# Encoder layer on one core: standing zeros beside the queries, sums of squares in one column, eps as a column

## The chip, the cores and the metric

The kernel runs on one core of one Trainium2 chip. The metric is the time of one execution in device microseconds; the kernel before takes 1554.6 us (median of 3 runs, 1553.99 to 1555.76).

## What is computed

One layer of an encoder on x of 1024 tokens by 1024 channels, in float32. The part that the change touches is the differential attention (8 heads, two softmax maps a head, a head size of 64 for queries and keys, 128 for values):

```python
def head_rmsnorm(x, g):
    xf = x.astype(jnp.float32)
    return xf * lax.rsqrt(jnp.mean(xf * xf, axis=-1, keepdims=True) + EPS) * g.astype(jnp.float32)
...
    qn = head_rmsnorm(q, g_q) * (HEAD_DIM ** -0.5)
    kn = head_rmsnorm(k, g_k)
...
        s = jnp.einsum('bqhid,bkhid->bihqk', qblk, kn)
...
        s = jnp.where(allowed, s + bias, neg)
        p = jax.nn.softmax(s, axis=-1)
        a = p[:, 0] - lam * p[:, 1]
        return jnp.einsum('bhqk,bkhe->bqhe', a, vf)
...
    o = head_rmsnorm(o, g_sub) * (1.0 - lambda_init)
```

Ahead of it stand an RMSNorm and one projection to q, k, v and the pooling's channels; beside it a pooling mixer and the gates; behind it the branch products, the output projection and an MLP of 4096 channels with a squared ReLU.

## The kernel before

**Numbers in two halves.** Most matmuls work on fp32r operands. `split` (L115) makes two tiles of a float32 one: ScalarE casts the high half, VectorE (or GpSimd) subtracts it to give the low half. `mm3` (L120) then issues three matmuls, high by high, high by low and low by high, from the lines L123, L124 and L125. Nearly every projection in the trace is made of these three lines.

**Attention as a pipeline.** The tokens are 8 tiles of 128, so that 8 heads give 64 tiles, numbered g = 8h + t. For each g the loop at L645 runs stages of several tiles at once, each with its own lag (L48). `A` (`stage_qkv`) projects one tile into `z` in PSUM: 24 matmuls of 384 columns. `B` (`stage_prep`) squares q and k on ScalarE (L436), sums each of the four blocks of 64 on VectorE (L437), turns the sums into means with eps (L248) and takes the power -0.5 on GpSimd (L249); VectorE scales q and k (L441), GpSimd multiplies k by the gains (L447). `C` (`stage_qkT`) transposes them (L459, tile `tk`) and fills K and Q. The weights of a scores matmul have 128 rows for a head size of 64: the rows of one half hold q's high part against k's high part, the rows of the other half meet k's low part. So Q of each map is two tiles of weights: in the first, q's high part (L470) on its own rows and q's low part (L471) on the others; in the second, q's low part (L472) on its own rows and q (L473) on the others. `D` computes scores and softmax (tiles `sc`, `s`; L499 to L524), `E` transposes the weights of the values (tile `ta`, L555), `F` (`stage_pv`) multiplies them by V into the output `po` in PSUM, for a pair of tiles (256 queries) at a time, and stores it to DRAM unscaled.

**The sums of squares of the output.** ScalarE squares `po` into `oq` (L579), and `split` makes `oqs` of it, two halves. One step later `H` (`stage_ssq`) multiplies a 128x128 tile of ones by each half (L590, L591), 256 columns each, into the unused half of `po`'s bank. Each of the 128 rows of the result is then the same sum over the channels, and L593 takes its diagonal out with `identf`, one column of SS for each of the two tiles. `R` (`stage_norm`) makes the scales of a head from SS; they go to DRAM and are multiplied into the outputs when these are loaded for the branch product.

**Filling work.** The gates' columns (tile `g`) and the pooling's groups (`u`, `yp`) depend only on the normed x. They are written behind the attention in the code; the scheduler of the language, which runs a model of the engines, fills them in between the attention's instructions. A pooling group projects 512 tokens (`u`), copies the result to SBUF (L710), adds it to itself shifted by 1, 2, 4, 8 (L719; GpSimd copies the first columns, L718), subtracts (L728), splits (`mix`), and after one unit of the gates multiplies by the group's matrix (`yp`). A gate column loads its weights with two DMAs on SyncE's queue (`frgate`).

**Behind the attention** come the branch products (`bp`, `ba`), the output projection (`op`) and the MLP, which takes 7 products of half matrices in place of 8 (`X`, `Y`, `Z`, `W`, `Da`, `Db`). The change touches none of their lines.

Of the kernel before, what the change touches and what calls it, by code (L numbers as in the profile page):

```python
# [8 lines left out]
F32 = mybir.dt.float32  # L9
F32R = mybir.dt.float32r  # L10
I32 = mybir.dt.int32
AF = mybir.ActivationFunctionType
ALU = mybir.AluOpType
AX = mybir.AxisListType
# [3 lines left out]
P = 128  # L18
S = 1024
D = 1024  # L20
NT = S // P
NK = D // P
H = 8
HD = 64
POOLD = 512
WINDOWS = (2, 4, 8, 16)
EPS = 1e-6
# [7 lines left out]
N_Q, N_QN = 3, 2  # L35
# [20 lines left out]
def encoder_kernel(  # L56
# [21 lines left out]
    nc = tc.nc  # L78
    x, out = x[0], out[0]
# [4 lines left out]
    const = ctx.enter_context(tc.tile_pool(name="const", bufs=1))  # L84
# [15 lines left out]
    def htile(shape, dt, name, th):  # L100

        if th == 0:
            hcount[0] += 1
        return (hp1 if th else hp0[(hcount[0] - 1) // 4 % 2]).tile(shape, dt, tag="H", name=name)
# [7 lines left out]
    def f(ap):  # L112
        return ap.bitcast(F32)

    def split(hi, lo, src, lo_eng=None):  # L115

        nc.scalar.copy(hi, src)  # L117
        return (lo_eng or nc.vector).tensor_tensor(lo, src, f(hi), op=ALU.subtract)  # L118

    def mm3(ps, lhs_hi, lhs_lo, rhs_hi, rhs_lo, first, last, more=False):  # L120

        kw = {"skip_group_check": True} if more else {}
        nc.tensor.matmul(ps, lhs_hi, rhs_hi, start=first, stop=False, **kw)  # L123
        nc.tensor.matmul(ps, lhs_hi, rhs_lo, start=False, stop=False, **kw)  # L124
        nc.tensor.matmul(ps, lhs_lo, rhs_hi, start=False, stop=last, **kw)  # L125
# [101 lines left out]
    identf = const.tile([P, P], F32, name="identf")  # L227
    make_identity(nc, identf)
    mhalf = const.tile([P, NT], F32, name="mhalf")
    nc.gpsimd.memset(mhalf, -0.5)  # L230
    ones = const.tile([P, P], F32R, name="ones")
    nc.gpsimd.memset(f(ones), 1.0)
    inv = const.tile([P, 16], F32, name="inv")
    for i in range(16):
        nc.gpsimd.memset(inv[:, i : i + 1], 1.0 / (i + 1))
# [10 lines left out]
    def rsq(dst, ss, n, c):  # L246

        nc.vector.tensor_scalar(dst, ss, c, EPS, op0=ALU.mult, op1=ALU.add)  # L248
        nc.gpsimd.tensor_tensor(dst, dst, mhalf[:, :n], op=ALU.pow)  # L249
# [39 lines left out]
    with ExitStack() as ph:  # L289
        sp = ph.enter_context(tc.tile_pool(name="sp", bufs=1))  # L290
# [4 lines left out]
        def s1(shape, dt, name, tag, bufs=1):  # L295
            return sp.tile(shape, dt, tag=tag, name=name, bufs=bufs)
# [70 lines left out]
        gqk = sp.tile([P, 2, HD], F32, name="gqk")  # L367
        nc.sync.dma_start(gqk[:, 0, :], g_q[0].partition_broadcast(P))
        nc.sync.dma_start(gqk[:, 1, :], g_k[0].partition_broadcast(P))
        lqk = s1([P, 4, HD], F32, "lqk", "oq")  # L370
        nc.sync.dma_start(lqk, lambda_qk[0].partition_broadcast(P))

        dist = sp.tile([P, S], F32, name="dist")
# [13 lines left out]

        def small_params():
            nc.vector.scalar_tensor_tensor(
                gg, gqk[:, 0, :], HD ** -0.5, gqk[:, 1, :], op0=ALU.mult, op1=ALU.mult  # L390
            )
            nc.vector.tensor_tensor(lp, lqk[:, 0:4:2, :], lqk[:, 1:4:2, :], op=ALU.mult)
            nc.vector.tensor_reduce(ls, lp, axis=AX.X, op=ALU.add)
            nc.scalar.activation(ls, ls, AF.Exp)
            nc.vector.scalar_tensor_tensor(
                nlam, ls[:, 1:2], -LAMBDA_INIT, ls[:, 0:1], op0=ALU.add, op1=ALU.subtract
            )

        gg = sp.tile([P, HD], F32, name="gg")
# [4 lines left out]
        st = {}  # L404
        ATs = {}
        Zs = {}
        SS = {}

        gghs = {}

        def head_start(h):
            gghs[h] = sp.tile([P, HD], F32, tag="ggh", name=f"ggh{h}", bufs=2)
            nc.gpsimd.tensor_scalar(gghs[h], gg, -(2.0 ** (h + 1)), None, op0=ALU.mult)
            kv_tiles(h)
            Zs[h] = sp.tile([P, 2, NT], F32, tag="Z", name=f"Z{h}", bufs=2)
            SS[h] = sp.tile([P, NT], F32, tag="SS", name=f"SS{h}", bufs=2)
# [13 lines left out]
        def stage_prep(h, t):  # L430
            th = t // 4
            V, ggh = KV[h][1], gghs[h]
            z = st[h, t]["z"]
            sq = s1([P, 256], F32, f"sq{h}_{t}", "sq")
            ms = sp.tile([P, 4], F32, tag="ms", name=f"ms{h}_{t}", bufs=3)
            nc.scalar.activation(sq, z[:, 0:256], AF.Square)  # L436
            nc.vector.tensor_reduce(ms, sq.rearrange("p (a b) -> p a b", a=4), axis=AX.X, op=ALU.add)  # L437
            rsq(ms, ms, 4, 1.0 / HD)
            split(V[th][:, t % 4, 0, :], V[th][:, t % 4, 1, :], z[:, 256:384])
            qn = s1([P, 4, HD], F32, f"qn{h}_{t}", "qn", N_QN)  # L440
            nc.vector.tensor_tensor(  # L441
                qn,
                z[:, 0:256].rearrange("p (a b) -> p a b", a=4),
                ms.unsqueeze(2).broadcast_to([P, 4, HD]),
                op=ALU.mult,
            )
            nc.gpsimd.tensor_tensor(  # L447
                qn[:, 2:4, :], qn[:, 2:4, :], ggh.unsqueeze(1).broadcast_to([P, 2, HD]), op=ALU.mult
            )
            st[h, t] = {"qn": qn}  # L450
            yield

        def stage_qkT(h, t):

            th, c0 = t // 4, (t % 4) * P
            K, qn = KV[h][0][th], st[h, t]["qn"]
            tr = ps_t.tile([P, 512], F32, tag="tr", name=f"tk{h}_{t}")
            for i in range(2):
                nc.tensor.transpose(  # L459
                    tr[:, i * P : (i + 1) * P], qn[:, 2 * i : 2 * i + 2, :].rearrange("p a b -> p (a b)"), identf  # L460
                )
            Q = sp.tile([P, 2, 2, P], F32R, tag="Q", name=f"Q{h}_{t}", bufs=N_Q)
            halves = (slice(0, HD), slice(HD, P))
            for m in range(2):
                own, other = halves[m], halves[1 - m]
                q, k = tr[own, 0:P], tr[own, P : 2 * P]
                k_hi, q_hi = K[own, m, c0 : c0 + P], Q[own, m, 0, :]
                nc.scalar.copy(k_hi, k)
                nc.vector.tensor_tensor(K[other, m, c0 : c0 + P], k, f(k_hi), op=ALU.subtract)  # L469
                nc.scalar.copy(q_hi, q)  # L470
                nc.vector.tensor_tensor(Q[other, m, 0, :], q, f(q_hi), op=ALU.subtract)  # L471
                nc.vector.tensor_tensor(Q[own, m, 1, :], q, f(q_hi), op=ALU.subtract)  # L472
                nc.scalar.copy(Q[other, m, 1, :], q)  # L473
            st[h, t]["Q"] = Q
            yield

        def stage_scores(h, t):

            K, Q = KV[h][0], st[h, t]["Q"]
            n = (t + 1) * P  # L480
# [84 lines left out]
        def stage_pv(h, p):  # L565
            V, views = KV[h][1], ATs.pop((h, p))[0]
            po = ps_o.tile([P, 512], F32, tag="o", name=f"po{h}_{p}")
            nkt = 2 * p + 2
            for kt in range(nkt):
                v = V[kt // 4]  # L570
                mm3(
                    po[:, 0:256], v[:, kt % 4, 0, :], v[:, kt % 4, 1, :],
                    views[kt][0], views[kt][1], kt == 0, kt == nkt - 1,
                )
                if kt % 2 and kt < nkt - 1:
                    yield
            oS = s1([P, 256], F32, f"oS{h}_{p}", "oS", 2)
            oq = s1([P, 256], F32, f"oq{h}_{p}", "oq")
            nc.scalar.activation(oq, po[:, 0:256], AF.Square)  # L579
            nc.scalar.copy(oS, po[:, 0:256])  # L580
            nc.scalar.dma_start(y_dram[h * P : (h + 1) * P, p * 256 : (p + 1) * 256], oS)
            oqs = s1([P, 2, 256], F32R, f"oqs{h}_{p}", "oqs")
            split(oqs[:, 0, :], oqs[:, 1, :], oq)
            st[h, p, "o"] = (po, oq, oqs)
            yield

        def stage_ssq(h, p):

            po, oq, oqs = st.pop((h, p, "o"))
            nc.tensor.matmul(po[:, 256:512], ones, oqs[:, 0, :], start=True, stop=False)  # L590
            nc.tensor.matmul(po[:, 256:512], ones, oqs[:, 1, :], start=False, stop=True)  # L591
            for i in range(2):
                nc.vector.tensor_tensor_reduce(  # L593
                    out=oq[:, i * P : (i + 1) * P], in0=po[:, 256 + i * P : 256 + (i + 1) * P], in1=identf,
                    scale=1.0, scalar=0.0, op0=ALU.mult, op1=ALU.add,
                    accum_out=SS[h][:, 2 * p + i : 2 * p + i + 1],
                )
            yield

        def stage_norm(h):  # L600
# [14 lines left out]
            yield  # L615

        small_params()
        N = H * NT

# [25 lines left out]
        for g in range(-2, N + 8):  # L645
# [11 lines left out]
            for tok in ORDER:  # L657
                if tok not in gens:
                    i = g - tok[1]
# [151 lines left out]
    for d in range(NK):  # L811
# [10 lines left out]
        for th in range(2):  # L822
# [5 lines left out]
            t = htile([P, 2, 512], F32R, f"mT{d}_{th}", th)  # L828
# [495 lines left out]
```

## Time and profile before

| what | value |
| --- | --- |
| median of 3 runs | 1554.6 us |
| the profiled execution | 1553.41 us, its span 1551.6 us |
| granted TensorE clock | 1.00 |
| TensorE busy: matmul, weight load | 1533.6 us, 1320.8 us |
| VectorE, ScalarE, GpSimd busy | 1011.3, 816.7, 354.8 us |
| DMA | 206.94 MB, 133 GB/s in the mean |

The attention with its filling work lies from about 12 to 700 us, the branch products from 700 to 850, output projection and MLP behind that.

How to read it: PE is a matmul on TensorE, PEld its weight load, which can run beside the matmul before. DVE is VectorE, ACT ScalarE, POOL GpSimd, SP SyncE's queue. L590 is a line of the kernel. A group's row has line, engine, operation, output and inputs, shapes and count, then busy us and the mean ns of one, then the idle time of the engine ahead of them and what ended it. A row of the timeline has start, duration, engine, line. The end of a matmul is modelled and matmuls overlap, so that the step from one start to the next says what one costs in a dense stretch. A row of the waits has the total in us, how many, the longest.

### The profile page before, as it was taken

The page shows a single profiled execution, that of the slowest core. Times are in us where ns is not written, and L with a number is a line of the kernel's source. Part 1 is how long each engine was busy: PE and PEld are TensorE (multiplying, and loading weights), DVE is VectorE, ACT ScalarE, POOL GpSimd, SP SyncE. Part 2 cuts the span into 40 slices and gives each one's busy share as a digit, 9 for nine tenths or more (in the row PEclk, how much of TensorE's full clock was granted, in tenths as well). Part 3 has the DMA queues.
Part 4 walks back from the last instruction along what each step waited for, and adds up shares of the span by engine and source line. Part 5 has one row for each costly group of instructions (what it writes and reads, how often), then busy time and mean ns, then how long its engine had stood idle before and what let it go on. Part 6 is the DMA issues. An engine that isn't in the chain of part 4 may idle for free.

```text
span 1551.6 us, 22088 instructions
## 1 busy us (share of the span) xinstructions
PE 1533.6 (99%) x7649; PEld 1320.8 (85%) x7649; DVE 1011.3 (65%) x2277; ACT 816.7 (53%) x1810; POOL 354.8 (23%) x449
## 2 busy tenths in 40 slices
PE   7999999999999999999999999999999999999999
PEld 6999999999998989888888887888888788888887
DVE  7777677777878787746422458866665667556662
ACT  6656556656566555645532547565555633333331
POOL 5433334243525262324363400000000000000000
PEclk9999999999999999999999999999999999999999
DMA  7111212021202031248536534554343799437650
GB/s 229 51 53 48 66 41 68 24 75 37 75 28 83 28 96 42 69 147 284 179 122 210 168 112 124 182 185 155 129 142 109 278 334 370 170 122 257 224 190 27
DMA packets 168009, 206.94 MB, mean 133 GB/s; under 512 B 10117, under 2 KB 104026, under 8 KB 167898
## 3 DMA queue, kind: packets, MB, share of 16 engines
q1 hardware_dynamic: 150490, 178.23, 35.0%
q10 hardware_dynamic: 17408, 27.30, 4.7%
q8 instruction: 60, 0.98, 0.3%
q14 instruction: 51, 0.42, 0.1%
HBM read 150.94 MB, written 54.56 MB: 132 GB/s over the span
## 4 chain that ended last, share of the span: by engine, by line
PE 89%; DVE 4%; DMA 3%; ACT 1%; issue 1%; POOL 1%; SPq 0%; ACTq 0%; POOLq 0%; DVEq 0%
PE z L125 5%; PE z L123 5%; PE z L124 5%; PE Da L124 4%; PE Da L123 4%; PE Da L125 4%; PE g L123 3%; PE g L124 3%; PE g L125 3%; PE Db L124 3%; PE Db L123 3%; PE Db L125 3%; PE X L125 2%; PE X L123 2%; PE X L124 2%; PE sc L499 2%
## 5 line engine op out<-in xcount | busy, mean ns | idle before, releaser
L123 PE MATMUL z<-wqkv,hT 128*128 128x384 f32 x512 | 174.7, 342 | 0.4 <-DVE qn L441 0.3
L125 PE MATMUL z<-wqkv,hT 128*128 128x384 f32 x512 | 174.3, 341 | 0.5 <-DVE hT L118 0.5
L124 PE MATMUL z<-wqkv,hT 128*128 128x384 f32 x512 | 173.8, 339 | 0.0
L510 ACT ACTIVATE s<-s,nm 128x256 f32<-128x256 f32 (+7 forms) x128 | 99.6, 778 | 49.2 <-DVE nm L502 44.1
L249 POOL TENSOR_TENSOR ms<-ms,mhalf 128x4 f32<-128x4 f32 x64 | 66.6, 1040 | 157.7 <-DVE ms L248 139.1
L125 PE MATMUL g<-hT,fwgate 128*128 128x512 f32 x256 | 101.0, 394 | 0.0
L124 PE MATMUL g<-hT,fwgate 128*128 128x512 f32 x256 | 100.9, 394 | 0.0
L123 PE MATMUL g<-hT,fwgate 128*128 128x512 f32 x256 | 100.9, 395 | 0.0
L123 PEld LDWEIGHTS z<-wqkv,hT 128*128 128x128 f32 x512 | 96.9, 189 | 4.2 <-DVE qn L441 1.0
L125 PEld LDWEIGHTS z<-wqkv,hT 128*128 128x128 f32 x512 | 96.7, 189 | 3.3 <-DVE hT L118 1.3
L124 PEld LDWEIGHTS z<-wqkv,hT 128*128 128x128 f32 x512 | 96.8, 189 | 2.9
L502 DVE CUSTOM_DVE_ANT_0 s<-sc,dist 128x512 f32<-128x512 f32 (+3 forms) x128 | 74.7, 586 | 22.1 <-PE sc L500 20.7
L118 POOL TENSOR_TENSOR wqkv<-rqkv,wqkv 128x384 fp32r<-128x384 f32 x60 | 63.3, 1072 | 17.7 <-ACT wqkv L117 15.3
L499 PE MATMUL sc<-K,Q 128*128 128x512 f32 (+2 forms) x192 | 67.2, 355 | 0.1
L118 DVE TENSOR_TENSOR AS<-s,AS 128x512 fp32r<-128x512 f32 x64 | 43.8, 687 | 35.8 <-ACT AS L117 35.6
L500 PE MATMUL sc<-K,Q 128*128 128x512 f32 (+2 forms) x192 | 66.6, 354 | 0.0
L473 ACT CAST Q<-tk 64x128 fp32r<-64x128 f32 x128 | 33.2, 260 | 58.6 <-DVE Q L472 56.8
L447 POOL TENSOR_TENSOR qn<-qn,ggh 128x128 f32<-128x128 f32 x64 | 32.6, 510 | 137.5 <-DVE qn L441 124.2
L470 ACT CAST Q<-tk 64x128 fp32r<-64x128 f32 x128 | 33.1, 259 | 50.5 <-DVE K L469 49.1
L118 POOL TENSOR_TENSOR fwgate<-frgate,fwgate 128x512 fp32r<-128x512 f32 x32 | 45.2, 1416 | 52.2 <-ACT fwgate L117 52.0
L125 PEld LDWEIGHTS g<-hT,fwgate 128*128 128x128 f32 x256 | 48.1, 188 | 8.6
L123 PEld LDWEIGHTS g<-hT,fwgate 128*128 128x128 f32 x256 | 48.2, 188 | 7.1
(429 smaller groups left out, 4649.6 us busy)
## 6 DMA issues: line engine op xcount, KB each, us to landing
wd<-in_w_down_dram SPq DMA_DIRECT2D x56, 512.0 KB, 5.5
wu<-in_w_up_dram SPq DMA_DIRECT2D x32, 512.0 KB, 5.3
udS<-us SPq DMA_DIRECT2D x64, 256.0 KB, 2.5
ur<-udS SPq DMA_DIRECT2D x32, 512.0 KB, 3.2
rqkv<-in_w_in_dram SPq DMA_DIRECT2D x64, 192.0 KB, 2.8
ud<-u ACTq DMA_DIRECT2D x48, 256.0 KB, 2.2
ur<-ud SPq DMA_DIRECT2D x24, 512.0 KB, 5.5
frgate<-in_w_gate_dram SPq DMA_DIRECT2D x32, 256.0 KB, 2.6
```

Source lines behind the costliest of these rows:

```text
L118: return (lo_eng or nc.vector).tensor_tensor(lo, src, f(hi), op=ALU.subtract)
L123: nc.tensor.matmul(ps, lhs_hi, rhs_hi, start=first, stop=False, **kw)
L124: nc.tensor.matmul(ps, lhs_hi, rhs_lo, start=False, stop=False, **kw)
L125: nc.tensor.matmul(ps, lhs_lo, rhs_hi, start=False, stop=last, **kw)
L249: nc.gpsimd.tensor_tensor(dst, dst, mhalf[:, :n], op=ALU.pow)
L447: nc.gpsimd.tensor_tensor(qn[:, 2:4, :], qn[:, 2:4, :], ggh.unsqueeze(1).broadcast_to([P, 2, HD]), op=ALU.mult)
L470: nc.scalar.copy(q_hi, q)
L473: nc.scalar.copy(Q[other, m, 1, :], q)
L499: nc.tensor.matmul(dst, Q[:, i, 0, :], rhs, start=True, stop=False)
L500: nc.tensor.matmul(dst, Q[:, i, 1, :], rhs, start=False, stop=True)
L502: nc.vector.tensor_tensor_reduce(out=s[i][:, c : c + w], in0=sc[:, 0:w], in1=dist[:, o0 + c : o0 + c + w], scale=2.0 ** -(h + 1), scalar=B ...
L510: nc.scalar.activation(s[i][:, 0:n], s[i][:, 0:n], AF.Exp, bias=last, scale=-1.0, accum_out=Z[:, i, t : t + 1])
```

## The change

It makes three edits.

- **Queries.** Q is no longer taken from a pool: three tiles `Q0` to `Q2` live through the whole attention and are used in turn. In the first tile of weights the rows of the other half are set to zero once by GpSimd, and no instruction writes them again; the product of the two low halves (L471) is left out of the scores.
- **Squares of q and k.** They are written into a standing tile of four blocks of 65 columns, of which the last holds 64 eps from the start. The sum over 65 columns then has eps in it, and GpSimd takes the power of the sum, not of the mean: the instruction of L248 goes for these 64 tiles. The factor 64 that this leaves in q times k stands in the gains (`HD ** 0.5` in place of `HD ** -0.5`).
- **Squares of the output.** `oq` is no longer split. Each of its two 128x128 blocks is the weights of a plain float32 matmul whose moving operand is one column of ones, so that the sum arrives as one column, with queries on the partitions. ScalarE copies the two columns to SS. `oq` has two buffers, `oqs` is gone, and so are the products with the tile of ones and the diagonal sums.

```diff
-    ones = const.tile([P, P], F32R, name="ones")
-    nc.gpsimd.memset(f(ones), 1.0)
+    ones = const.tile([P, 1], F32, name="ones")
+    nc.gpsimd.memset(ones, 1.0)
...
-        lqk = s1([P, 4, HD], F32, "lqk", "oq")
+        lqk = s1([P, 4, HD], F32, "lqk", "oq", 2)
...
-                gg, gqk[:, 0, :], HD ** -0.5, gqk[:, 1, :], op0=ALU.mult, op1=ALU.mult
+                gg, gqk[:, 0, :], HD ** 0.5, gqk[:, 1, :], op0=ALU.mult, op1=ALU.mult
...
+        sq = sp.tile([P, 4, HD + 1], F32, name="sq")
+        nc.gpsimd.memset(sq[:, :, HD : HD + 1], HD * EPS)
+        Qs = [sp.tile([P, 2, 2, P], F32R, name=f"Q{i}") for i in range(N_Q)]
+        halves = (slice(0, HD), slice(HD, P))
+        for Q in Qs:
+            for m in range(2):
+                nc.gpsimd.memset(f(Q[halves[1 - m], m, 0, :]), 0.0)
...
-            sq = s1([P, 256], F32, f"sq{h}_{t}", "sq")
-            nc.scalar.activation(sq, z[:, 0:256], AF.Square)
-            nc.vector.tensor_reduce(ms, sq.rearrange("p (a b) -> p a b", a=4), axis=AX.X, op=ALU.add)
-            rsq(ms, ms, 4, 1.0 / HD)
+            nc.scalar.activation(sq[:, :, 0:HD], z[:, 0:256].rearrange("p (a b) -> p a b", a=4), AF.Square)
+            nc.vector.tensor_reduce(ms, sq, axis=AX.X, op=ALU.add)
+            nc.gpsimd.tensor_tensor(ms, ms, mhalf[:, 0:4], op=ALU.pow)
...
-            Q = sp.tile([P, 2, 2, P], F32R, tag="Q", name=f"Q{h}_{t}", bufs=N_Q)
-            halves = (slice(0, HD), slice(HD, P))
+            Q = Qs[(NT * h + t) % N_Q]
...
-                nc.vector.tensor_tensor(Q[other, m, 0, :], q, f(q_hi), op=ALU.subtract)
...
-            oq = s1([P, 256], F32, f"oq{h}_{p}", "oq")
+            oq = s1([P, 256], F32, f"oq{h}_{p}", "oq", 2)
...
-            oqs = s1([P, 2, 256], F32R, f"oqs{h}_{p}", "oqs")
-            split(oqs[:, 0, :], oqs[:, 1, :], oq)
-            st[h, p, "o"] = (po, oq, oqs)
+            st[h, p, "o"] = (po, oq)
...
-            po, oq, oqs = st.pop((h, p, "o"))
-            nc.tensor.matmul(po[:, 256:512], ones, oqs[:, 0, :], start=True, stop=False)
-            nc.tensor.matmul(po[:, 256:512], ones, oqs[:, 1, :], start=False, stop=True)
+            po, oq = st.pop((h, p, "o"))
             for i in range(2):
-                nc.vector.tensor_tensor_reduce(
-                    out=oq[:, i * P : (i + 1) * P], in0=po[:, 256 + i * P : 256 + (i + 1) * P], in1=identf,
-                    scale=1.0, scalar=0.0, op0=ALU.mult, op1=ALU.add,
-                    accum_out=SS[h][:, 2 * p + i : 2 * p + i + 1],
+                nc.tensor.matmul(
+                    po[:, 256 + i : 257 + i], oq[:, i * P : (i + 1) * P], ones, start=True, stop=True
                 )
+            nc.scalar.copy(SS[h][:, 2 * p : 2 * p + 2], po[:, 256:258])
```

Because the scheduler places the filling work by its model of the engines, the three edits also change the order of the first 700 us on every engine; behind the branch products the order is the same but for the numbers of buffers. Two places on TensorE show it.

The first is the sum of squares of the first output pair (head 0, tiles 0 and 1). Before, TensorE's rows there are:

```order
L499 MATMUL sc_4_0_0_945<-K_0_357,Q_4_796 128x512
L590 MATMUL po_0_826<-oqs_0_838,ones 128x256
L499 MATMUL sc_4_0_512_960<-K_1_358,Q_4_796 128x256
L123 MATMUL z_0_1060<-wqkv_3_856,hT_0_0_143 128x384
L125 MATMUL g_0_7202<-hT_0_0_147,fwgate_1_7199 128x512
L124 MATMUL z_0_1060<-wqkv_3_856,hT_0_0_143 128x384
L591 MATMUL po_0_826<-oqs_0_838,ones 128x256
L125 MATMUL z_0_1060<-wqkv_3_856,hT_0_1_144 128x384
```

In the changed kernel, where the sum of squares is L598, they are:

```order
L123 MATMUL g_0_6765<-hT_0_0_143,fwgate_0_6757 128x512
L470 MATMUL tk_5_901<-identf,qn_5_777 128x128 x2
L598 MATMUL po_0_810<-ones,oq_0_818 128x1 x2
L124 MATMUL z_0_1030<-wqkv_1_828,hT_0_0_141 128x384
L125 MATMUL z_0_1030<-wqkv_1_828,hT_0_1_142 128x384
L508 MATMUL sc_4_0_0_920<-K_0_368,Q_237 128x512
```

The two products of 256 columns, with other matmuls between them, have become two of one column that follow each other.

The second place is the last product of the pooling (`yp` of the fourth group, second half). Before, it stands in the middle of the attention of the last head:

```order
L123 MATMUL z_5_6608<-wqkv_7_5908,hT_1_0_327 128x384
L124 MATMUL z_5_6608<-wqkv_7_5908,hT_1_0_327 128x384
L500 MATMUL sc_1_0_0_6486<-K_0_6088,Q_1_6385 128x256
L125 MATMUL z_5_6608<-wqkv_7_5908,hT_1_1_328 128x384
L123 MATMUL yp_1_8245<-mix_1_8204,wgrp_8082 128x512
L124 MATMUL yp_1_8245<-mix_1_8204,wgrp_8082 128x512
L125 MATMUL yp_1_8245<-mix_1_8204,wgrp_8082 128x512
L499 MATMUL sc_1_1_0_6509<-K_0_6088,Q_1_6385 128x256
```

In the changed kernel the attention is over by then, and gates stand on both sides:

```order
L123 MATMUL g_0_7780<-hT_0_0_147,fwgate_1_7777 128x512
L124 MATMUL g_0_7780<-hT_0_1_148,fwgate_1_7777 128x512
L125 MATMUL g_0_7780<-hT_0_0_147,fwgate_1_7777 128x512
L123 MATMUL yp_1_7808<-mix_1_7767,wgrp_7645 128x512
L124 MATMUL yp_1_7808<-mix_1_7767,wgrp_7645 128x512
L125 MATMUL yp_1_7808<-mix_1_7767,wgrp_7645 128x512
L123 MATMUL g_1_7815<-hT_1_0_332,fwgate_0_7772 128x512
L124 MATMUL g_1_7815<-hT_1_1_333,fwgate_0_7772 128x512
```

Ahead of this `yp` stand exactly the 24 rows of one unit of the gates (`g`), and ahead of those the `u` from which `mix` is made; before, pieces of attention lay between `u` and `yp` as well.

## The prediction

> **What bounds the kernel now.** I read the page first, then the stages, then what TensorE waits for.
>
> ```profile
> span 1551.6 us, 22088 instructions
> PE 1533.6 (99%) x7649; PEld 1320.8 (85%) x7649; DVE 1011.3 (65%) x2277; ACT 816.7 (53%) x1810; POOL 354.8 (23%) x449
> PE 89%; DVE 4%; DMA 3%; ACT 1%; issue 1%; POOL 1%; SPq 0%; ACTq 0%; POOLq 0%; DVEq 0%
> ```
>
> TensorE is busy for 99% of the span and holds 89% of the chain that ended last. Its busy time alone proves little, because matmuls overlap; so I go on to the stages (start:end, length, then busy us and count of PE, PEld, DVE, ACT, POOL, then the granted clock).
>
> ```profile
> 12.00:50.00 38.00, 37.55 (x212) 34.16 (x213) 31.93 (x84) 25.89 (x69) 21.06 (x25) 1.00 0.52 166
> 50.00:700.00 650.00, 648.02 (x3712) 593.20 (x3712) 482.26 (x1534) 389.64 (x1116) 239.38 (x326) 1.00 0.20 62
> 850.00:1551.60 701.60, 695.30 (x3070) 569.80 (x3068) 431.85 (x572) 330.30 (x508) 19.55 (x20) 1.00 0.53 183
> ```
>
> All edits lie in the first 700 us. There TensorE is idle for 650.00 - 648.02 = 2.0 us after the start-up, at full clock (1.00). What it waits for in the whole run:
>
> ```profile
> PE hps L275 <- DVE hn L270: 8.8, 1, 8.8
> PE X L123 <- ACT U L1075: 2.0, 2, 1.3
> PE ta L555 <- DVE AT_0l L118: 1.0, 1, 1.0
> PE ta L555 <- DVE AT_4l L118: 0.6, 1, 0.6
> PE z L123 <- DVE qn L441: 0.3, 1, 0.3
> ```
>
> The 8.8 us are the first loads and the X wait is in the MLP: neither is touched. What relief of VectorE and ScalarE can win is 1.0 + 0.6 + 0.3 = 1.9 us. So the sum is made of TensorE's own work, and its price is the step from one matmul's start to the next:
>
> ```profile
> 232.44 0.40 PE L123 MATMUL g<-hT,fwgate 128*128 128x512 f32 x1
> 232.68 0.28 PE L590 MATMUL po<-oqs,ones 128*128 128x256 f32 x1
> 232.80 0.39 PE L499 MATMUL sc<-K,Q 128*128 128x512 f32 x1
> ...
> 233.50 0.28 PE L591 MATMUL po<-oqs,ones 128*128 128x256 f32 x1
> 233.61 0.33 PE L123 MATMUL z<-wqkv,hT 128*128 128x384 f32 x1
> ```
>
> 512 columns take a step of 0.24 us, the 256 columns of a sum of squares 0.12 and 0.11 us. The 0.28 in the second column is a modelled end and no price.
>
> **The change, part by part.** *The removed products.* L590 and L591 run once for each of 32 output pairs: 32 x (0.12 + 0.11) = **7.4 us** of TensorE's time go.
>
> *The added products.* Each pair now has two plain float32 products with a 128x128 block of squares as weights and one moving column. The compiled program holds 7713 weight loads and 7713 matmuls where it held 7649 of each; so each of the 64 products stands as two load-and-matmul passes, four passes a pair. With one column nothing hides the load of the next pass. The order has the two products side by side in 26 of 32 pairs. No plain float32 product is in this trace, so its load is bounded by two others:
>
> ```profile
> L123 PEld LDWEIGHTS z<-wqkv,hT 128*128 128x128 f32 x512 | 96.9, 189 | 4.2 <-DVE qn L441 1.0 <-ACT hT L117 0.6
> L555 PEld LDWEIGHTS ta<-identf,s 128*128 128x128 f32 x288 | 35.8, 140 | 7.5 <-PE g L125 2.4
> L611 PEld LDWEIGHTS trr<-identf,r 128*8 128x8 f32 x8 | 0.7, 84 | 0.2
> ```
>
> The last two differ by 120 columns and 56 ns: 0.47 ns a column, **0.06 us** for 128 columns of a float32 transpose, on a fixed delay of about 80 ns. Against the same delay the fp32r load of the first row takes (189 - 80) = **0.11 us**. That can be seen where the array had run dry after a wait:
>
> ```profile
> 560.31 0.19 PEld L123 LDWEIGHTS z<-wqkv,hT 128*128 128x128 f32 x1
> 560.42 0.19 PEld L124 LDWEIGHTS z<-wqkv,hT 128*128 128x128 f32 x1
> 560.60 0.19 PEld L125 LDWEIGHTS z<-wqkv,hT 128*128 128x128 f32 x1
> ```
>
> Two loads with nothing to hide behind stand 0.11 us apart; the next comes a 384-column matmul later (0.18). In a pair the first load hides beside the matmul ahead of it, as L590's did. Three loads between the passes stand bare, and so does that of the matmul that follows, an fp32r one at 0.11. The three are 0.06 to 0.11 each: 0.29 to 0.44 us a pair. I take one kind of each in a product, 0.11 + 0.06 + 0.11, and 0.11 behind: 0.39 us, x 32 = **12.5 us** (9.3 to 14.1). Net: 12.5 - 7.4 = **+5.1 us** (+1.9 to +6.7).
>
> The Trainium skill (TensorE: Matmul & The Clock Gate, section LDWEIGHTS) puts a load at its columns over 1.2 GHz, whatever the rows: 107 ns for 128. The fp32r step of 0.11 agrees; the transposes' 0.06 does not. By the page alone a pair would cost 4 x 0.107 = 0.43 us, and the net would be +6.3 us, an estimate within my ends.
>
> *What VectorE and ScalarE lose.*
>
> ```profile
> L471 DVE TENSOR_TENSOR Q<-tk,Q 64x128 fp32r<-64x128 f32 x128 | 37.0, 289 | 20.2 <-ACT Q L470 17.1
> L248 DVE TENSOR_SCALAR ms<-ms 128x4 f32<-128x4 f32 x64 | 16.2, 253 | 0.6
> L593 DVE CUSTOM_DVE_ANT_0 oq<-po,identf 128x128 f32<-128x128 f32 x64 | 16.1, 284 | 3.0 <-PE po L591 2.8
> L118 DVE TENSOR_TENSOR oqs<-oq,oqs 128x256 fp32r<-128x256 f32 x32 | 17.3, 541 | 4.1 <-ACT oqs L117 3.4
> L117 ACT CAST oqs<-oq 128x256 fp32r<-128x256 f32 x32 | 13.2, 411 | 0.2
> ```
>
> The low half of q under its zeros (L471), the eps step, the diagonal sums and the split of the squares are 37.0 + 16.2 + 16.1 + 17.3 = 86.6 us of VectorE, and 13.2 us of ScalarE, which gets 32 copies of 128x2 in exchange (none is in the trace: above nothing, below the 411 ns of this wide cast, so at most as much as it lost). All of it lies beside TensorE, which waited for it 1.9 us in all. I count **0**, with -1.9 as the end. The new copy holds the output's only PSUM bank until it has run; by the order at least 3.5 us of TensorE's work stand between a pair's sums and the next writer of that bank, so 0.4 us are covered; if that cover went, it would be 32 x 0.4 = 13 us. Squares written with a gap, 65 columns summed in place of 64 and eps as a constant column are the same instructions on the same engines: 0. A power of a sum in place of a mean has no row of its own; GpSimd is 37% busy in that stage, so 0.
>
> *The seven new memsets* (six of 64x128 zeros, one eps column) stand on GpSimd behind `rows`:
>
> ```profile
> 1.93 0.20 POOL L362 MEMSET rows<- 32x128 f32 x1
> 7.40 0.56 POOL L264 TENSOR_TENSOR rs<-rs,mhalf 128x1 f32<-128x1 f32 x1 [5.27 <-DVE rs L263]
> ```
>
> At 0.20 each they take 1.4 us of an idle stretch of 5.27 us ahead of the first power: 0. Without that gap they would delay the start by 1.4 us.
>
> *What is moved.* The scheduler, seeing VectorE freer, runs attention ahead of the filling work: the last z matmul is the 3322nd instead of the 3556th, and 343 rows of gates and pooling stand behind the last sum of squares, where 34 did. With them move their loads on SyncE's queue, two a column:
>
> ```profile
> frgate<-in_w_gate_dram SPq DMA_DIRECT2D x32, 256.0 KB, 2.6
> ```
>
> A column is 48 matmuls, 11 us at 0.23, for two loads of 2.6 us, so the weights keep up, and their stores follow the evictions on ScalarE's queue as before: 0. But the pooling's chain loses its cover. Between a `u` product and its `yp` the order of before has at least 12 us of TensorE's work (by the steps above); now the last four have 8.3, 6.9, 5.6 and 5.5 us. In that time must run:
>
> ```profile
> L710 ACT COPY u<-u x8: 566/588/592, 294.0 to 575.1; 128x512 f32<-128x512 f32 x8
> L719 DVE TENSOR_TENSOR sum<-u x8: 678/710/1795, 294.6 to 577.1; 128x511 f32<-128x511 f32 x4, 128x527 f32<-128x527 f32 x4
> L719 DVE TENSOR_TENSOR sum<-sum x12: 683/724/1475, 391.8 to 582.5; 128x510 f32<-128x510 f32 x3, 128x526 f32<-128x526 f32 x3, 128x508 f32<-128x508 f32 x2, 128x524 f32<-128x524 f32 x2
> L728 DVE SCALAR_TENSOR_TENSOR sum<-sum,u x8: 679/718/1653, 295.6 to 584.7; 128x512 f32<-128x512 f32 x4, 128x511 f32<-128x511 f32 x1, 128x509 f32<-128x509 f32 x1, 128x505 f32<-128x505 f32 x1
> L117 ACT CAST mix<-sum x8: 605/621/644, 296.4 to 585.9; 128x512 fp32r<-128x512 f32 x8
> L118 DVE TENSOR_TENSOR mix<-sum,mix x8: 674/684/1051, 297.1 to 587.0; 128x512 fp32r<-128x512 f32 x8
> ```
>
> For the window of 16: 0.59 + 0.71 + 3 x 0.72 + 0.72 + 0.62 + 0.68 = 5.5 us without the handing over between engines, against 5.6 and 5.5 us of cover. I put the deficit at 0.7 us for each of the two, about **+1.5 us** (0 if the minima hold, 4 if the other two wait for a laden VectorE as well).
>
> **Sum.** +5.1 + 1.5 = +6.6 us. The profiled execution took 1553.41 us around its span of 1551.6, so it would become 1560.0; the median of the runs is 1.2 us above it (1554.6), which gives **1561.2 us**. With all ends: 1554.6 + 1.9 - 1.9 = 1554.6 to 1554.6 + 6.7 + 4 = 1565.3.
>
> **Rivals.**
> *Cheap loads*: all bare loads take 0.06 us, also that behind the pair, and nothing waits in the tail: 0.24 x 32 = 7.7 us for 7.4; up to 1.9 us of old waits go. 1553 to 1556.
> *Faster*: the small products cost nothing because their loads run several ahead behind the long matmuls; it decides if a pair costs under 0.13 us (a gain of 3.1 us). At nothing: 1554.6 - 7.4 = 1547.2. Against it: in the rows of 560 us a load starts only when the one before it is through.
> *Packed attention*: its steps stand closer, and TensorE waits for the chain of scores, exponents and transposes 0.1 us a step, 64 steps: 1561.2 + 6.4 = 1567.6. Against it: VectorE falls from 482 of 650 us (74%) to some 396 of 596 (66%; 234 filling matmuls of 0.23 us leave).
> *Dear passes*: each load is paid with its fixed delay, 0.19 us: 4 x 0.19 x 32 = 24.3, net +16.9, with the tail 1573.0.
> *Four passes a product*: eight bare loads a pair, 0.88 x 32 = 28.2, net +20.8, 1576.9. The Trainium skill (FP8 and Floating Point Precision, section TensorE Precision Notes) counts four passes for true float32; the compiled program has two loads a product, which speaks against four loads.
>
> **How the numbers follow.** Forecast 0.60, cheap loads 0.15, faster 0.09, packed attention 0.09, dear passes 0.05, four passes 0.02. 0.2% is 3.1 us, about what a measurement of this kernel can tell from no change. Slower by more (above 1557.7): nine tenths of the forecast's 0.60, with the last three, 0.70; within it 0.06 + 0.15 = 0.21; faster 0.09. The range leaves out the faster case and the two dearest: 1553 to 1569.
>
> **What would show it.** The stage up to the branch products should hold 2 us less idle time at most; each pair of L598 should step by 0.3 to 0.44 us to the next matmul (below 0.23 the forecast's main term is wrong); VectorE should lose some 86 us; `yp` should wait for `mix` twice near the end of the filling work. A wait of TensorE for `po`, or a step of 0.7 us, would refute the sum.

## Result and profile after

The changed kernel takes **1577.16 us** (median of 4 runs, 1574.88 to 1579.63), the kernel before beside it 1555.18 us. The ratio is 1.014 with a 95% interval of 1.012 to 1.0159: 22.0 us slower. The prediction had the direction, and a size of 6.6 us.

The profiled execution took 1577.1 us. Of its page, the span, the engines and the chain that ended last:

```profile
span 1575.3 us, 21905 instructions
...
PE 1549.7 (98%) x7713; PEld 1328.0 (84%) x7713; DVE 936.4 (59%) x1925; ACT 814.5 (52%) x1810; POOL 356.0 (23%) x456
...
PE 91%; DMA 3%; ACT 2%; DVE 2%; issue 1%; SPq 0%; POOL 0%; ACTq 0%; DVEq 0%; POOLq 0%
```

VectorE has lost 75 us of busy time (the rows named in the prediction, 86.6 us, are gone; `mp` and `yT` in the branch products take 7.9 us more, and the rest is spread over many rows). TensorE has gained 16 and is still the bound. The stages of the changed kernel, in the columns of the prediction:

```profile
12.00:50.00 38.00, 37.60 (x211) 34.11 (x212) 30.03 (x81) 25.86 (x71) 20.05 (x25) 1.00 0.52 168
50.00:700.00 650.00, 641.17 (x3703) 586.03 (x3702) 397.76 (x1181) 379.57 (x1102) 239.07 (x325) 1.00 0.18 55
850.00:1575.30 725.30, 717.99 (x3142) 583.64 (x3140) 436.95 (x579) 332.24 (x512) 23.32 (x23) 1.00 0.54 184
```

The idle time of TensorE in the attention has grown from 2.0 to 650.00 - 641.17 = 8.8 us. What it waits for in the changed kernel:

```profile
PE hps L275 <- DVE hn L270: 8.9, 1, 8.9
PE X L123 <- ACT U L1079: 2.7, 2, 2.1
PE g L123 <- ACT go L749: 2.4, 4, 0.8
PE u L123 <- ACT yps L741: 1.0, 1, 1.0
PE g L123 <- ACT u L714: 1.0, 2, 0.7
PE trr L615 <- POOL r L613: 0.9, 1, 0.9
PE X L125 <- DVE AS L118: 0.9, 1, 0.9
PE yp L123 <- ACT go L749: 0.8, 1, 0.8
PE g L123 <- ACT yps L741: 0.8, 1, 0.8
```

The old waits for `AT` have shrunk from 1.6 us to 0.5 (0.3 and 0.2, the second below the rows shown). New are waits of filling work for ScalarE's copies out of PSUM (`go`, `u`, `yps`): 2.4 + 1.0 + 1.0 + 0.8 + 0.8 = 6.0 us. Three places in the trace show where time went.

**The products.** One output pair's four passes of L598, in the timeline of TensorE:

```profile
214.61 0.34 PE L123 MATMUL z<-wqkv,hT 128*128 128x384 f32 x1
214.79 0.50 PE L598 MATMUL po<-ones,oq 128*128 128x1 f32 x4
215.15 0.43 PE L124 MATMUL z<-wqkv,hT 128*128 128x384 f32 x1
215.41 0.34 PE L125 MATMUL z<-wqkv,hT 128*128 128x384 f32 x1
```

From the first pass to the next `z` are 0.36 us, and that `z` then steps by 0.26 where it steps by 0.18 (214.61 to 214.79). In ns the steps are 28, 112 and 111 from pass to pass and 112 to `z`, and in most pairs the step behind is 84 longer than it is elsewhere: 28 + 112 + 111 + 112 + 84 = 447 ns, or 0.447 us a pair. The loads of the second to fourth pass and of the next two `z` start 109, 112, 112 and 111 ns apart. So a pair costs the time of four bare loads of 0.11 us each, with no cheaper one among them; the load of the first pass was hidden. In the 6 pairs whose two products stand apart, a product costs half of it, some 0.22 us.

**The tail of gates.** Two engines, at one change of a gate's tile:

```profile
667.10 0.39 PE L125 MATMUL g<-hT,fwgate 128*128 128x512 f32 x1
667.53 0.69 ACT L749 ACTIVATE go<-g,cols 128x512 f32<-128x512 f32 x1 [5.36 <-PE g L125]
...
668.26 0.50 PE L123 MATMUL g<-hT,fwgate 128*128 128x512 f32 x1 [0.78 <-ACT go L749]
```

A bank is here a tile of 512 float32 columns in PSUM, where TensorE puts its results. The last matmul into the bank starts at 667.10; ScalarE, idle for 5.36 us, empties the bank at once, and the next tile begins only then: 1.16 us from start to start in place of 0.23. `u`, `yp` and the gates below column 13 all use one PSUM bank (the pool `ps_f` has one). While there was attention to interleave, its matmuls covered this: the kernel before shows no wait for `go`, `u` or `yps`. Behind the attention nothing covers it. The waits also touch the clock (the last column but two):

```profile
650.30:653.80 3.50, 1.90 (x8) 0.94 (x7) 0.69 (x1) 1.73 (x3) 0.00 (x0) 0.99 0.63 224
653.80:657.20 3.40, 3.40 (x9) 2.62 (x9) 0.00 (x0) 0.00 (x0) 0.00 (x0) 0.50 0.23 83
```

After 3.5 us in which TensorE was idle for 1.6, the granted clock is 0.50 for 3.4 us: 9 matmuls that step by some 0.43 us in place of 0.23, which costs some 1.7 us.

**The last stage.** Nothing in the MLP was changed, but it is slower. TensorE in the same 240 us of the down products, before, then after (count in brackets):

```profile
1262.00:1502.00 240.00, 240.00 (x1051) 1.00 0.68 236
```

```profile
1262.00:1502.00 240.00, 240.00 (x1030) 1.00 0.70 241
```

No wait and no lower clock, but 21 matmuls fewer: 233 ns a step in place of 228. From the first to the last, the 1344 matmuls of `Da` and `Db` take 313.4 us in place of 307.4, 6.0 us more. What differs is the place: the room of the ones shrank from 512 to 32 bytes a partition, and so the tiles behind it stand 480 bytes lower. (Addresses in this document are those of the program; the traces hold none.)

### The profile page after: what moved, and what is told of

Read it like the earlier page. It is cut to its first block, busy times and chain, and to the rows that moved or that the text cites. A ratio compares the mean times of both kernels' runs of the same rounds, so it can differ in the third digit from the quotient of the medians.

```text
span 1575.3 us, 21905 instructions
## 1 busy us (share of the span) xinstructions
PE 1549.7 (98%) x7713; PEld 1328.0 (84%) x7713; DVE 936.4 (59%) x1925; ACT 814.5 (52%) x1810; POOL 356.0 (23%) x456
## 4 chain that ended last, share of the span: by engine, by line
PE 91%; DMA 3%; ACT 2%; DVE 2%; issue 1%; SPq 0%; POOL 0%; ACTq 0%; DVEq 0%; POOLq 0%
PE z L125 5%; PE z L123 5%; PE z L124 5%; PE Da L124 4%; PE Da L123 4%; PE g L123 4%; PE Da L125 4%; PE g L124 4%; PE g L125 4%; PE Db L124 3%; PE Db L123 3%; PE Db L125 3%; PE X L125 2%; PE X L123 2%; PE X L124 2%; PE sc L508 2%
## 5 line engine op out<-in xcount | busy, mean ns | idle before, releaser
L449 POOL TENSOR_TENSOR ms<-ms,mhalf 128x4 f32<-128x4 f32 x64 | 70.7, 1104 | 156.0 <-DVE ms L447 153.2
L123 PEld LDWEIGHTS g<-hT,fwgate 128*128 128x128 f32 x256 | 48.4, 189 | 15.3 <-ACT go L749 3.9
L125 PEld LDWEIGHTS g<-hT,fwgate 128*128 128x128 f32 x256 | 48.5, 190 | 9.0
L479 DVE TENSOR_TENSOR K<-tk,K 64x128 fp32r<-64x128 f32 x128 | 36.9, 288 | 31.9 <-ACT K L478 28.2
L124 PEld LDWEIGHTS g<-hT,fwgate 128*128 128x128 f32 x256 | 48.5, 189 | 8.1
```

What stands on the lines that cost most here:

```text
L449: nc.gpsimd.tensor_tensor(ms, ms, mhalf[:, 0:4], op=ALU.pow)
```

## Experiments

The theory with which the first runs were made: the products cost some 6.5 us (four loads of 0.11 us in place of 0.235 us of products a pair), the waits of moved filling work 5 to 9, the placement 5 to 7. The rival: the relief of VectorE and the moved order act as a whole, through attention's own chains.

### Placement

**a1_ones_room** keeps all edits and reserves the old room for the ones:

```diff
-    ones = const.tile([P, 1], F32, name="ones")
+    ones = const.tile([P, P], F32, name="ones")[:, 0:1]
```

> The changed kernel, with the column of ones in a tile as wide as before (128 columns reserved, one used), so that every later tile in SBUF lies where it lay before; the order of instructions is that of the changed kernel, row for row. Theory (placement): the last stage of the MLP (tiles Da and Db, 1344 matmuls) took 307.4 us before and 313.4 after with the same instructions in the same order, because the operands moved by 480 bytes; with the room restored it goes back to 307, and the kernel is 5 to 7 us faster than the changed one, some 1571. Rival (the run, not the place: clock or chance): the stage stays at 313 and the time at 1577.

Measured 1570.38 us (1569.79 to 1570.87), ratio to before 1.01 (1.0084 to 1.0116): 6.8 us below the changed kernel, with the same order of instructions. The last stage is back to 1050 matmuls:

```profile
1262.00:1502.00 240.00, 240.00 (x1050) 1.00 0.71 245
```

**a2_before_pad32** puts 32 bytes into the constants of the kernel before:

```diff
+    pad = const.tile([P, 8], F32, name="pad")
+    nc.gpsimd.memset(pad, 0.0)
     inv = const.tile([P, 16], F32, name="inv")
```

> The kernel before, with a tile of 32 bytes more ahead of the later tiles, which it never reads; order as before. Theory (placement): the moving operands of the last stage then start at a multiple of 64 bytes, as in the changed kernel, in place of 32 behind one; the stage takes about 313 us in place of 307 and the kernel is 5 to 7 us slower than before. Rival (the run): no difference, within 1 us. Rival (distance, not the place within 64 bytes: it is the move by 480 bytes that counts): no difference either, while the run with the room restored still gains.

Measured 1560.93 us, ratio 1.0041 (1.0026 to 1.0057). The same 240 us in its trace:

```profile
1262.00:1502.00 240.00, 240.00 (x1030) 1.00 0.68 234
```

The loss of the last stage comes without any of the three edits: 1030 matmuls, as in the changed kernel. So it is placement, and no part of the change's arithmetic.

Which placement? The steps of all stages, grouped by the addresses of their operands, suggested that what counts is whether the moving operand and the weights that load beside it start at the same place modulo 512, and not the start modulo 64, which would have explained a1 and a2 as well. **b3_places_512** tells the two apart:

```diff
-    ones = const.tile([P, P], F32, name="ones")[:, 0:1]
+    ones = const.tile([P, 112], F32, name="ones")[:, 0:1]
```

> The changed kernel with 448 bytes reserved for the column of ones, where a1_ones_room reserved 512: every tile behind it stands 64 bytes lower, TensorE's order is the same instruction by instruction. Theory (a step costs least, 227 ns, when the moving operand and the weights that load beside it start at the same place modulo 512 bytes): the two halves of the MLP's down products then stand at 480 and 480 and step 227 in place of 229 ns (1344 x 2.2 = 3.0 us), B1 and B2 in X and Y stand as their weights and step 227 in place of 233.5 (384 x 6.6 = 2.5): 5.5 us less than a1, 1565 us. Rival (only the start modulo 64 counts, which 64 bytes leave as it is): the time of a1, 1570.4.

Measured 1564.37 us (1563.38 to 1565.68), ratio 1.0064 (1.0051 to 1.0077).

```profile
1262.00:1502.00 240.00, 240.00 (x1060) 1.00 0.71 244
```

1060 matmuls, more than before's 1051; the steps of `X` and `Y` with `B1` and `B2` fell from 233 to 227 ns too. With the start modulo 64 unchanged, this refutes the rival. It does not tell 512 from 256 (see the last section).

### The tail's bank

**b1_tail_banks**, on a1:

```diff
-G_FIRST, G_Z = 13, 13
+G_FIRST, G_Z = 13, 10
...
-            ps = fill_proj(ws, th, f"u{g}_{th}")
+            ps = fill_proj(ws, th, f"u{g}_{th}", spare_bank if (g, th) == (3, 1) else fill_bank)
...
-            ps = ps_f.tile([P, 512], F32, tag="f", name=f"yp{g}_{th}")
+            ps = (spare_bank if g == 3 else fill_bank)(f"yp{g}_{th}")
```

> The changed kernel with the place of all tiles held (as a1_ones_room, 1570.4 us, whose TensorE order it keeps up to the last head), and one more edit: from gate column 10 on, the last u and the last two yp take their PSUM bank in turn from three banks, where they all went through one. Theory (the tail of gates waits for the eviction of its only bank, 0.8 to 1.0 us at each change of the bank's user, and the idle time also sets off 3.4 us at half clock): these waits go, 5.5 to 6.5 us of the tail's 7.8, and with them the half-clock stretch, 1.7: 1562 to 1565 us. Rival (the tail waits for weights or for the pooling's chain on VectorE and ScalarE, and the bank is only the last of several): 2 us or less goes, 1568 to 1571.

Measured 1562.43 us (1561.96 to 1562.75), ratio 1.005 (1.0035 to 1.0066): 8.0 us below a1. The stretch from 629 to 700 us, in a1 and in b1:

```profile
629.00:700.00 71.00, 64.59 (x270) 50.65 (x270) 10.70 (x17) 17.07 (x29) 22.64 (x22) 0.98 0.26 84
```

```profile
629.00:700.00 71.00, 69.38 (x308) 56.99 (x307) 12.39 (x21) 19.95 (x34) 22.73 (x22) 1.00 0.32 104
```

4.8 us less idle, full clock, 38 matmuls more. The filling work behind the last sum of squares, 342 matmuls in both traces, steps by 256 ns in the mean in a1 and by 232 in b1, which makes 8.3 us. Of b1's waits:

```profile
PE yp L123 <- ACT mix L117: 1.3, 1, 1.3
...
PE g L123 <- ACT go L749: 0.5, 1, 0.5
...
PE g L123 <- ACT SS L601: 0.3, 1, 0.3
```

Now `yp` waits for `mix`, which the prediction had named: in the changed kernel the bank came free later still, 0.46 us after `mix` was done, and hid it.

### The products

**b2_one_product**, on a1, leaves out the second product of each pair, so that the second tile's sum of squares is missing:

```diff
-            for i in range(2):
-                nc.tensor.matmul(
-                    po[:, 256 + i : 257 + i], oq[:, i * P : (i + 1) * P], ones, start=True, stop=True
-                )
-            nc.scalar.copy(SS[h][:, 2 * p : 2 * p + 2], po[:, 256:258])
+            nc.tensor.matmul(po[:, 256:257], oq[:, 0:P], ones, start=True, stop=True)
+            nc.scalar.copy(SS[h][:, 2 * p : 2 * p + 2], po[:, 256:257].broadcast_to([P, 2]))
```

> The same held placement (a1_ones_room, 1570.4 us), with the second of the two one-column products of each output pair left out; the copy takes the first sum twice, so the second tile's sum of squares is missing. 32 products, 64 passes, go. Theory (every bare load behind a one-column pass takes 0.11 us, of either kind): 64 x 0.11 = 7.0 us less, 1563.4, give or take 2.5 since the scheduler also shortens the tail from 343 to 294 rows; in the trace a pair steps 0.22 us to the next matmul where it stepped 0.44. Rival of cheap loads (0.06): 3.8 us less. Rival of dear passes (0.19): 12.2 us less.

Measured 1563.09 us (1562.27 to 1565.04): 7.3 us below a1, where 0.11 a load gives 7.0, 0.06 gives 3.8 and 0.19 gives 12.2. Its timeline:

```profile
218.24 0.34 PE L124 MATMUL z<-wqkv,hT 128*128 128x384 f32 x1
218.41 0.28 PE L597 MATMUL po<-ones,oq 128*128 128x1 f32 x2
218.55 0.42 PE L125 MATMUL z<-wqkv,hT 128*128 128x384 f32 x1
218.81 0.34 PE L123 MATMUL z<-wqkv,hT 128*128 128x384 f32 x1
```

0.14 us to the next `z`, which steps by 0.26: half of the pair's price, by the steps 32 x 0.223 = 7.1 us. The total alone would prove less: b2's tail is shorter (294 rows for 343) and without a1's stretch at half clock, and it has a wait of 1.8 us for `s` that a1 has only at 0.3.

### The edits apart

**a4_columns_alone** is the kernel before with the third edit and the old room for the ones; **a3_without_columns** has the first two, with the sums of squares as before; **b4_eps_alone** and **c4_queries_alone** have one of these each. The edits are those of the diff above.

> The kernel before with the edit of the output's squares alone, the ones in a tile as wide as before. Theory: four loads of 0.11 us a pair in place of 0.235 us of products, +6.5 us, and 292 matmuls of filling work behind the attention with 5 to 9 us of waits: 11 to 16 us slower than before. Rival (the waits come from all three edits together): +6 to +8 us.

Measured 1572.37 us (1571.01 to 1572.63), ratio 1.0111 (1.0093 to 1.0129): a little over its range. Alone it costs 2.0 us more than all three edits together (a1); the executions of the two do not overlap, the intervals of their ratios do. Two waits on VectorE differ, in a4, then in a1:

```profile
PE ta L559 <- DVE AT_0l L118: 1.2, 2, 1.0
...
PE ta L559 <- DVE s L523: 1.2, 1, 1.2
```

```profile
PE ta L564 <- DVE AT_0l L118: 0.3, 1, 0.3
...
PE ta L564 <- DVE s L528: 0.3, 1, 0.3
```

So the other two edits may win back some 2 us here. The order differs as well, and no run tells relief from order.

> The changed kernel without the edit of the output's squares: split, two products of 256 columns and diagonal sums as before, standing zeros and eps column as changed. Theory (products and waits): TensorE's products cost as before, placement as before; the order puts 193 matmuls of filling work behind the attention (34 before, 343 after), so part of the waits stays: 2 to 5 us slower than before. Rival (relief): VectorE has 53 us less to do, the waits of before go, and it is 0 to 2 us faster than before.

Measured 1560.98 us (1560.28 to 1562.0), ratio 1.004 (1.0024 to 1.0056): slower by more than I expected, and no relief. Its loss and a4's, 6.2 and 17.5 us, are more than the 15.5 of a1, which has all three edits: what the edits cost through the order does not add up.

> The kernel before with the eps edit alone; placement as before, 46 rows of gates behind the last sum of squares where before had 34. Theory (VectorE's relief buys nothing, and what costs is the moved order, which this edit hardly moves): within 2 us of before, 1553 to 1557. Rival (the 64 instructions on VectorE's chain ahead of the transposes were a bound after all): 3 us or more faster, below 1552. Rival (the power of a sum in place of a mean, or the squares written with a gap, costs): above 1557.5.

Measured 1555.71 us (1554.65 to 1557.59), ratio 1.001 (1.0001 to 1.0019): the instruction that went from VectorE 64 times wins nothing.

> The kernel before with the standing zeros alone, places as before; the tail has 193 rows like a3_without_columns (1561.0 us) and not 46 like b4_eps_alone (1555.7). Theory (what decides is the order, and this edit alone makes it): most of a3's 6.2 us, 1558 to 1561. Rival (each edit costs by its own instructions, half and half): 1557.5 to 1558, or, if eps in a3 is the dearer, below.

Measured 1559.82 us (1558.27 to 1562.8), ratio 1.0038 (1.0025 to 1.0051): standing zeros alone make most of a3's loss, though they only take work away.

### Places and banks put right

**c1_before_places** is the kernel before with two pads:

```diff
+    gap = fq.tile([P, 96], F32, name="gap")
+    nc.vector.memset(gap, 0.0)
...
+    pad = const.tile([P, 112], F32, name="pad")
+    nc.gpsimd.memset(pad, 0.0)
```

> The kernel before, none of the three edits, with 448 bytes of padding in the constants' pool and 384 ahead of the attention's small tiles: nearly every moving operand then starts at the same place modulo 512 bytes as the weights that load beside it (480), where in before B1 and B2 (480 against 32), the down products (32 against 480) and the branch product of the attention (160 against 32) did not; TensorE's order is that of before. Theory (a step of 512 columns costs 227 ns when the two agree): down products 1344 x 2.2 = 3.0, B1 and B2 384 x 6.6 = 2.5, the branch product 384 x 6.5 = 2.5 us, 8.0 in all: 1546 to 1548 us, and a ba step of 227. Rival (the branch product's 229 and 238 ns have another cause, such as its weights' arrival): 5.5 us less, 1549.

Measured **1547.02 us** (1545.87 to 1548.57), ratio 0.9951 (0.9939 to 0.9963): faster than both kernels. TensorE in 80 us of the attention's branch product, before, then c1:

```profile
750.00:830.00 80.00, 80.00 (x344) 1.00 0.40 132
```

```profile
750.00:830.00 80.00, 80.00 (x354) 1.00 0.41 128
```

80 us over 354 are 226 ns, over 344 they are 233.

**c2_all_edits_places** has all edits, b1's banks, the gap of c1 and, in place of its second pad, the 448 bytes of b3 for the ones:

> All three edits, the three banks in the tail of b1_tail_banks, and the places of c1_before_places. Theory (banks, places and products add up and do not touch one another): 1562.4 of b1 less 8.0 for the places, 1553 to 1556 us, which is 7 us above c1 for the products (32 x 0.447 - 7.4 = +6.9) and nothing for the rest of the change. Rival (VectorE's relief is worth something once the waits are gone): under 1552, less than 5 us above c1.

Measured 1555.42 us (1553.48 to 1557.62), ratio to before 1.0004 (0.9996 to 1.0013), and 8.4 us above c1: the products' 6.9, 0.9 us in which `yp` still waits for `mix`, and 0.6 that I cannot place.

**c3_q_eps_places** leaves the sums of squares as before:

> The edits of queries and eps without the sums in a column, with the three banks in the tail and the places of c1. Theory (these two edits cost only through the tail's waits and the half-clock stretch they set off, some 4 us of the 6.2 that a3_without_columns showed, and win nothing): 1561.0 - 8.0 - 4 = 1549 us, 1547 to 1551, level with c1 or up to 3 us above it. Rival (freed VectorE wins time once nothing waits in the tail): below c1 by 2 us or more. Rival (the two edits slow something else by 6 us): 1552 or more.

Measured 1552.84 us (1550.51 to 1557.9), ratio 0.9993 (0.9983 to 1.0003): a miss, 5.8 us above c1 where I had 0 to 3, and in the range of the rival in which the two edits slow something else. The banks did little here; the largest loss lies in the attention itself. Of c3's waits, the stretches around the largest, and VectorE there:

```profile
PE z L125 <- DVE qn L456: 2.2, 1, 2.2
...
PE sc L512 <- DVE nm L515: 1.3, 3, 0.6
```

```profile
456.10:459.50 3.40, 1.19 (x8) 0.95 (x8) 2.29 (x7) 2.32 (x7) 0.58 (x2) 1.00 0.18 53
459.50:462.90 3.40, 3.40 (x13) 3.40 (x11) 1.49 (x5) 1.90 (x6) 2.79 (x5) 0.50 0.20 77
```

```profile
457.07 0.17 DVE L530 RECIPROCAL cf<-Z 128x1 f32<-128x1 f32 x1 [0.99 <-ACT s L523]
457.27 0.22 DVE L531 SCALAR_TENSOR_TENSOR cf<-cf,Z,nlam 128x1 f32<-128x1 f32 x1
457.53 0.89 DVE L532 SCALAR_TENSOR_TENSOR s<-s,cf,s 128x640 f32<-128x640 f32 x1
458.33 0.42 DVE L456 TENSOR_TENSOR qn<-z,ms 128x256 f32<-128x256 f32 x1
```

The next `z` needs the bank that `qn` reads. In the new order `qn` stands on VectorE's queue behind three instructions of a softmax that waits for ScalarE, while TensorE has no filling work next in its order: four transposes (`ta`) and then 2.2 us of nothing. The stretch at half clock follows the wait, and together they cost some 3.9 us of the 5.8. The rest stays open. c2 has the same two edits in another order and no wait for `qn`, which speaks for the order and not for the edits' own work; no run that holds the order with these two edits was made.

## Why the prediction was wrong

The direction was right; the 15.4 us that are missing come from these steps.

- **Removed products, 7.4 us**: right. In the trace of before 51 of the 64 step by 0.11 to 0.12 us, which would make 7.6 for all; the other 13 stand right behind a transpose and step by 0.20, which I put down to the transpose's load.
- **Added products, 12.5 us**: right in mechanism, too small. Measured 32 x 0.447 = 14.3, net +6.9 where I had +5.1, and just above my upper end of 14.1. The step that failed took one of the three loads between the passes at 0.06 us, worked out from the durations of transposes; all four loads take 0.11. The transposes themselves could have warned me: from one `ta` to the next, the trace of before has 0.109 us. The Trainium skill's rule (TensorE: Matmul & The Clock Gate, section LDWEIGHTS) would have been nearer: 107 ns for any load of 128 columns, measured 0.11 here.
- **Relief of VectorE and ScalarE, 0**: right as far as the runs show: b4 and c4 took work from VectorE and were not faster. Only a1 against a4 leaves room for some 2 us.
- **The copy to SS, the memsets, the power of the sum**: 0, right; one wait of 0.3 us for `SS` in the changed kernel and in b1.
- **Moved filling work**: the step that failed most. I asked whether the weights of the moved gates and the chain of the pooling keep up. The weights do: no wait names `fwgate`. But "their stores follow the evictions on ScalarE's queue as before: 0" left out that each eviction has to end before the same bank is filled again, some 0.8 us that the interleaved attention had covered. By b1 this is 8.0 us with the half clock, where I had 1.5 for the whole tail. The two waits of `yp` for `mix` were not there; one showed when the bank was freed, 1.3 us.
- **What the sum had no term for**: the addresses. 6.8 us come from a tile of constants that became smaller (a1), 6.0 of them in a stage that I had counted as untouched.

The three together: 6.9 + 8.0 + 6.8 = 21.7 of 22.0 us. That it closes so well is in part luck: the three come from runs whose executions scatter by 1 to 2 us, and a3, a4 and c3 show that the order can cost or save several us more.

**The rivals.** *Four passes a product*, with 1576.9, was within 0.3 us of the time, and that is chance: the trace has 128 passes of L598 for 64 products, two each. *Dear passes*, with 1573.0 the next nearest, is refuted by its mechanism: a bare load costs 0.112 and not 0.19 us. *Cheap loads* and *faster* are refuted by b2's steps. (My argument against *faster*, that in the rows of 560 us a load starts only when the one before is through, does not follow from the rows as they stand: they last 0.19 us and start 0.11 apart.) *Packed attention* had part of the truth, of another shape: not 0.1 us at each step, but in a3 and c3 a few waits, the longest 2.2 us, where no filling work stands next.

## What to carry to other kernels

When an edit lets a scheduler move filling work, ask of the moved work not only whether its inputs arrive but who else uses its output bank, and what covered the eviction until now. A product with one moving column costs its weight loads, here 0.11 us each and two for plain float32; two products of 256 columns that hide their loads were cheaper than four bare loads. And a changed tile size moves the addresses behind it: hold the addresses when you compare an edit (a1 against the changed kernel), and try them by themselves (c1 won 7.4 us with two pads and no other edit).

## What the hardware showed that I had not expected

- **Operand places.** In these runs a 512-column matmul steps by 227 ns when its moving operand and the weights loaded beside it start at the same place modulo 512 bytes (480 and 480 in b3; 32 and 32 in before's `Z` and `W`), and otherwise by 229 in the mean (32 against 480), by 233 in the mean (480 against 32; 64 against 480) or, alternating from step to step, by 229 and 238 (160 against 32, `ba` before). The rule is fitted to these pairs; b3 and c1 bore out what it forecast. The same holds modulo 256 in all these pairs, so no run tells the two apart, and why it holds is open.
- **Half clock after short waits.** 3.41 us at a granted clock of 0.50 followed windows of about 3.4 us in which TensorE was idle for 1.3 us (a4, busy 2.09 of 3.40) to 2.2 (c3, busy 1.19 of 3.40), no single wait being longer than 2.2 us. The same wait of 2.2 us set it off in c3 and not in a3 (busy 1.20 of 3.40, clock 1.00 behind it), so it is not sure in any one run; one execution of the changed kernel had a clock of 1.000 and a span of 1573.0 in place of 1575.3 us. The Trainium skill (TensorE: Matmul & The Clock Gate, section A second HAM failure mode: psum-queue depth-cycling) tells of small idle gaps between groups of matmuls that make the clock swing; the trace of the tail agrees in part: after gaps of 0.83 and 0.78 us the clock fell once, and b1 without these gaps kept 1.00, but b2 has gaps of 0.7 to 0.8 us in its tail and kept 1.00 too.
